# A two-layer decoder trunk: the second layer's gate is summed at the layer boundary, and the residual rows are made there

## Chip, cores and metric

The kernel runs on one core of a Trainium2 chip. The metric is the device time of one execution in microseconds (us), lower is better. TensorE (PE) does the matmuls, VectorE (DVE), ScalarE (ACT) and GpSimd (POOL) the element work, and SyncE's queue (SP) issues most transfers.

## What is computed

Two layers over one sequence of 1024 tokens of 1024 features. Each layer modulates its input by three rows made of a conditioning vector, projects it once for three groups of heads (latent attention A, dilated B, sparse C with an indexer), gates, projects back and normalizes:

```python
for l in range(DEPTH):
    mod = jax.nn.silu(c) @ w_ada[l] + b_ada[l]
    shift, scale, gate = jnp.split(mod, 3, axis=-1)
    h = x * (1.0 + scale[:, None, :]) + shift[:, None, :]
    (p_cq, p_ckv, p_kr, p_qb, p_kb, p_vb, p_qc, p_kc, p_vc,
     p_qi, p_ki, p_wi, p_gate) = jnp.split(h @ w_in[l], SPLIT_POINTS, axis=-1)
    ...
    y = jnp.concatenate([o_a, o_b, o_c], axis=-1) * jax.nn.silu(p_gate)
    sub = y @ w_out[l]
    x = layer_norm(ALPHA * x + (1.0 + gate[:, None, :]) * sub, ln_g[l], ln_b[l])
```

The gate is used only after the output projection of its layer. Layer 1's scale and shift are needed as layer 0's output is turned into layer 1's h.

## The kernel before

Every product is made of three or two matmuls on a high and a low part (`split_w` loads a weight tile, ACT rounds it to the high part, POOL subtracts for the low part, L196 to L198). h lies transposed in SBUF for the whole layer. A layer runs in this order in the code: `indexer` (keys of the indexer, then four query chunks, and the index scores, summed over eight heads by DVE into the tile `acc`), two latent projections, the dilated heads B with the other projections between them, `select` (a bitwise search for the 256th score on DVE and ACT), the sparse heads C, the latent attention `mla`, and `out_proj`. Before layer 1's `indexer` the values of its dilated heads are projected, token block by token block, from 7 down to 0 (`values_b` with `natural`).

Modulation. `begin` makes layer 0's scale and shift. The other four rows of numbers are made by `later(i, ring)`: i = 0 and 1 are the gates of layer 0 and 1, 2 and 3 layer 1's scale and shift. Each calls `ada`: a memset of an accumulator tile (from the ring G), a bias load, and eight times a load of 512 KB and a DVE multiply-add of 128x1024 (L261). A gate's accumulator is then summed over partitions by two half-row matmuls against ones, each copied out by ACT, and stored (`ada_row`, L273 to L275); scale and shift go through `part_sums` (L266). The list ADA says where in layer 0's indexer each one stands: ADA[0] ahead of the keys, ADA[1+j] behind the projection of query chunk j. Their weight loads use three buffers there (two pt, one bi).

Residual rows. Layer 1's residual is layer 0's normalized output times ln_g plus ln_b. `residual(i)` makes it for one token block: load x1_d into the single tile RES (L805), two POOL products of 128x1024 (L806, L807), store to xw_d (L808). The first one also loads LNG and LNB (L802, L803). The code calls it in `mla` of layer 1, two blocks behind each of the heads 0 to 3 (NRES). RES is also one of two buffers in which `out_proj` of layer 0 loads rows of x.

Order. The code's order is a rank, not the order of execution: the tile framework (`schedule_with_timeline_sim=True` in `kernel`) writes each engine's queue ahead of time by its own simulated clock, so an instruction far down in the code can stand early in a queue whose engine is free by that clock. On the chip each queue then runs strictly as written.

Slices of `acc` serve as buffers too: AC[0] to AC[3], 1024 columns each, hold rows in `out_proj` until their transposes (L890) have been read.

Of the kernel before, what the change touches and what calls it, by code (L numbers as in the profile page):

```python
# [8 lines left out]
F32 = mybir.dt.float32  # L9
# [13 lines left out]
NB = 8  # L23
# [20 lines left out]

NQ = ((2,2,3,4,6,6,6),(2,2,3,4,6,6,6))

ADA = ((0,),(1,),(2,),(3,),())

NPC = 2

# [10 lines left out]
KE = (1,1)  # L61

NPL = 2

NRES = ((0,0,0,0,0,0),(2,2,2,2,0,0))

EARLY = (2,2)
FB = ((0,2,4,0,2,0),(1,3,1,1,1,1))
# [40 lines left out]
def trunk(ctx: ExitStack, tc: tile.TileContext, a, out):  # L109
# [236 lines left out]
    def natural(tb, wk, n0, n, k0=0):  # L346

        ps = ps_p.tile([P, 512], F32, name="pj")
        tok = slice(tb * P, (tb + 1) * P)
        items = []  # L350
        for k, (wh, wl) in enumerate(wk):
            ah, al = HA[k0 + k]
            items += [(ah[:, tok], wh), (al[:, tok], wh), (ah[:, tok], wl)]
        chain(ps[:, :n], items)
        return ps
# [32 lines left out]
    def values_b(tb, ps):  # L388
        evac_v(ps, tb, 6, 0)
        dve.tensor_scalar(wi[:, tb, :], ps[:, 384:392], float(8 ** -0.5), 0.125, OP.mult, OP.mult)  # L390
# [293 lines left out]
    def mla(l, values):  # L684
        PR.tiles = PR3 + AC[1:4] + [AC[0]]
        place = [(4, 512), (4, 640), (3, 640), (4, 0), (3, 0), (2, 0), (1, 0), (0, 0)]
        turn = []
        for g in ORDA[l]:
            for qb in (2 * g, 2 * g + 1):
                if place[qb][0] not in turn:  # L690
                    turn.append(place[qb][0])

        def slots(h):

            rows = [PR.tiles[(5 * h + turn.index(i)) % len(PR.tiles)] for i, _ in place]
            return [r[:, o:o + (qb + 1) * P] for qb, (r, (_, o)) in enumerate(zip(rows, place))]


        s8 = [QK.next() for _ in range(8)]
        held[:] = s8  # L700
        KA = [s8[0:2], s8[4:6]]
        QA = Ring(s8[2:4] + s8[6:8])
        kr = WR.next()
        sp.dma_start(kr[64:96, :], kr_d)
        sp.dma_start(kr[96:112, :], kr_d[16:32, :])
        sp.dma_start(kr[112:128, :], kr_d[0:16, :])
        act.activation(KA[0][0][64:128, :], kr[64:128, :], AF.Copy)
        dve.tensor_tensor(KA[0][1][64:128, :], kr[64:128, :], bc(KA[0][0][64:128, :]), OP.subtract)
        for i in range(2):
            pool.dma_start(KA[1][i][0:64, :], KA[0][i][64:128, :])  # L710
        ct, kraw = BI.next(), BI.next()
        sp.dma_start(ct, a["rope"])
        RAW = Ring([scrf])

        def keys(p):
            wh, wl = split_w(a["wuk"][l, p], 256)

            def evac(half, cols, ps):
                dve.tensor_tensor(kraw[:, cols], ps, rb[half], OP.mult)
            project(wh, wl, 2, CK, evac)  # L720

        def key(h):
            e = h % 2
            rr = slice(0, 64) if e == 0 else slice(64, 128)
            act.activation(KA[e][0][rr, :], kraw[rr, :], AF.Copy)
            (pool if KE[l] else dve).tensor_tensor(KA[e][1][rr, :], kraw[rr, :], bc(KA[e][0][rr, :]), OP.subtract)

        def split_q(Q, raw, cols):
            act.activation(Q[0][:, cols], raw, AF.Copy)
            (dve if QE[l] else pool).tensor_tensor(Q[1][:, cols], raw, bc(Q[0][:, cols]), OP.subtract)  # L730

        def query(h):

            wh, wl = split_w(a["wuq"][l, h], 768)
            Q = [(QA.next(), QA.next()) for _ in range(2 if h == 4 else 1)]
            for e in range(len(Q)):
                q[h + e] = Q[e]

            def evac(half, cols, ps):
                c = ct[:, cols]  # L740
                for e in range(len(Q)):
                    raw = RAW.next()
                    n, r = (slice(64, 128), 0) if (h + e) % 2 else (slice(0, 64), 64)
                    own, other, both = slice(r, r + 32), slice(r + 32, r + 64), slice(r, r + 64)
                    if UE[l] & (1 if h < 4 else 2):
                        act.activation(raw[n], ps[n], AF.Copy)
                    else:
                        dve.tensor_copy(raw[n], ps[n])
                    if h < 2:
                        dve.tensor_tensor(raw[both], ps[both], c[both], OP.mult)  # L750
                    elif h < 4:
                        dve.tensor_tensor(raw[own], ps[own], c[own], OP.mult)
                        dve.tensor_tensor(raw[other], ps[own], c[other], OP.mult)
                    else:
                        sp.dma_start(raw[both], qr_d[both, cols])
                    split_q(Q[e], raw, cols)
                    if h in (2, 3):
                        t = RAW.next()
                        dve.tensor_tensor(t[own], ps[other], c[own], OP.mult)
                        dve.tensor_tensor(t[other], ps[other], c[other], OP.mult)  # L760
                        sp.dma_start(qr_d[both, cols], t[both])

            project(wh, wl, 6, CA, evac)

        q, y, rest = {}, {}, list(range(NB))
        keys(0)
        key(0)
        query(0)
        key(1)
        for i in range(1, NQ[l][0]):  # L770
            query(i)
        values(2, 4, 0)
        for h in range(6):
            if h % 2 == 0:
                y[h // 2] = G.next()
                sp.dma_start(y[h // 2], ga_d[h // 2])
            Kh, Kl = KA[h % 2]
            Qh, Ql = q[h]

            def done(g, yt=y[h // 2], yo=HA[h // 2], c=None):  # L780
                c = c or slice(g * 256, g * 256 + 256)
                act.activation(yo[0][:, c], yt[:, c], AF.Copy)
                pool.tensor_tensor(yo[1][:, c], yt[:, c], bc(yo[0][:, c]), OP.subtract)

            attend(f'A{h}', [(Qh, Kh), (Ql, Kh), (Qh, Kl)], vblk((h + 4) % 6), None, scq, y[h // 2],
                   (h % 2) * 64, ORDA[l], done if h in (3, 5) else None, PACK[l] and slots(h))
            if h < 4:
                if h % 2 == 0:
                    keys(h // 2 + 1)
                    if h == 2:  # L790
                        done(0, y[0], HA[0], slice(0, 1024))
                key(h + 2)
            for i in range(NQ[l][h], NQ[l][h + 1]):
                if i < 5:
                    query(i)
            for _ in range(NRES[l][h]):
                residual(rest.pop(0))

    def residual(i):

        if i == 0:
            sp.dma_start(LNG, a["ln_g"][0].to_broadcast([P, 1024]))  # L802
            sp.dma_start(LNB, a["ln_b"][0].to_broadcast([P, 1024]))  # L803
        tb = TBO[i]
        sp.dma_start(RES, x1_d[tb])  # L805
        pool.tensor_tensor(RES, RES, LNG, OP.mult)  # L806
        pool.tensor_tensor(RES, RES, LNB, OP.add)  # L807
        sp.dma_start(xw_d[tb], RES)  # L808
# [159 lines left out]
    for l in range(DEPTH):  # L968
        layer[0] = l
        indexer(l)  # L970
        jobs = [lambda i=i: latent(l, i) for i in range(8)] + [lambda i=i: gate_a(l, i) for i in range(3)]
        values = None
        rb.clear()

        def fill_b(h):
            for _ in range(FB[l][h]):
                jobs.pop(0)()

        def fill_c(h):
            nonlocal values  # L980
            for _ in range(FC[l][h]):
                jobs.pop(0)()
            if h == 1:
                assert not jobs
                values = latents_back(l)

        for _ in range(EARLY[l]):
            jobs.pop(0)()
        heads_bc(l, BQK, 6, GB, 3, fill_b)
        select(l)  # L990
        if NPC:
            PR.tiles = PR.tiles + [BI.tiles[1], BI.tiles[0]][:NPC]
        heads_bc(l, CQK, 4, GC, 6, fill_c, extra=lambda: values_c(l))
        mla(l, values)
        out_proj(l)
        if l + 1 < DEPTH:
            wv = stage_vb(l + 1, Ring(held[4:8] + PT.tiles + [fresh("pr2", F32R), fresh("pr1", F32R)]))
            for tb in TBO:
                values_b(tb, natural(tb, wv, 0, 392))
            PR3[1:] = [fresh(f"pr{i}", F32) for i in (1, 2)]  # L1000
            PR.tiles = PR3[:]
            BI.tiles[1] = fresh("bi1", F32)
            RW.tiles = [fresh(f"rw{i}", F32, 512) for i in range(2)]
            G.tiles = [fresh(f"g{i}", F32) for i in range(2)]


def consts():
# [78 lines left out]
```

## Time and profile before

| | us |
|---|---|
| median of 3 runs | 1750.54 (1749.58 to 1754.23) |
| the profiled execution's own time | 1750.43 |
| its span, first to last instruction | 1748.6 |
| PE busy | 1673.0 (96%) |
| DVE busy | 1350.5 (77%) |
| ACT busy | 1019.8 (58%) |
| POOL busy | 666.9 (38%) |
| mean granted TensorE clock | 0.985 |

All rows below are of that execution; times in them are us from the span's start. The first layer's index stage runs from about 62 to 200, the layer boundary lies at about 896, and the second layer's index stage runs from 935 to 1055.

### The profile page before, as it was taken

To read this page: it belongs to the slowest core of one execution; us is meant where nothing else is said; L and a number is where in the kernel's file an instruction comes from. 1 tells how busy PE (TensorE), PEld (TensorE's weight loads), DVE (VectorE), ACT (ScalarE), POOL (GpSimd) and SP (SyncE) were. 2 spreads that over 40 slices of the span, in tenths; PEclk is the share of its full clock that TensorE was granted. 3 is DMA by queue.
4 is the path that set the end of the run, shared out by engine and by line. 5 is a ranking of instruction groups with operands and counts; after the bars stand their busy time and mean duration, and the time that the engine had idled before them with its cause. 6 is when DMAs were issued, how large, how long until landed. Compare 5 with 4: busy or idle time off the path is not lost.

```text
span 1748.6 us, 26930 instructions
## 1 busy us (share of the span) xinstructions
PE 1673.0 (96%) x9192; PEld 1451.5 (83%) x9192; DVE 1350.5 (77%) x3213; ACT 1019.8 (58%) x2010; POOL 666.9 (38%) x614
## 2 busy tenths in 40 slices
PE   8999899999999999989999999999999899998998
PEld 8888688888887888878898977888789788987886
DVE  6888898888588678885772668889876967778777
ACT  4254599895534666675112656999744357667620
POOL 0221143323434355463346413333243344657421
PEclk9999999999999999999999999999999999999999
DMA  9665023233202521222343421333221227113122
GB/s 367 212 215 189 25 73 97 70 136 91 79 35 54 221 90 58 73 70 93 125 157 124 168 73 49 85 111 95 73 97 50 60 52 265 47 52 124 49 86 95
DMA packets 57668, 187.32 MB, mean 107 GB/s; under 512 B 7862, under 2 KB 8886, under 8 KB 57020
## 3 DMA queue, kind: packets, MB, share of 16 engines
q1 hardware_dynamic: 53116, 156.25, 26.3%
q0 software_dynamic: 4416, 29.36, 5.8%
q8 instruction: 72, 1.18, 0.3%
q14 instruction: 64, 0.52, 0.1%
HBM read 133.94 MB, written 39.07 MB: 99 GB/s over the span
## 4 chain that ended last, share of the span: by engine, by line
PE 53%; DVE 8%; ACT 3%; issue 2%; DMA 1%; POOL 1%; DVEq 0%; ACTq 0%; POOLq 0%
PE pj L204 30%; PE S L204 12%; PE O L332 5%; PE T L320 5%; DVE pt L324 1%; ACT pt L323 1%; PE T L204 1%; ACT scr L485 1%; DVE acc L543 0%; DVE pr L536 0%; DVE acc L441 0%; PE T L890 0%; DVE h L818 0%; DVE acc L291 0%; ACT pr L296 0%
## 5 line engine op out<-in xcount | busy, mean ns | idle before, releaser
L204 PE MATMUL pj<-h,w 128*128 128x512 f32 (+1 forms) x3408 | 833.0, 391 | 13.9 <-DVE qk L238 5.8
L204 PEld LDWEIGHTS pj<-h,w 128*128 128x128 f32 x3408 | 629.9, 190 | 131.1 <-issue 11.9
L198 POOL TENSOR_TENSOR w<-wr,w 128x1024 fp32r<-128x1024 f32 (+2 forms) x86 | 192.4, 2238 | 302.3 <-ACT w L197 290.1
L204 PE MATMUL S<-qk,qk 128*128 128x512 f32 (+2 forms) x1104 | 279.7, 358 | 8.4 <-DVE mx L288 3.1
L323 ACT ACTIVATE pt<-T 128x512 fp32r<-128x512 f32 (+1 forms) x320 | 172.4, 551 | 111.2 <-PE T L320 53.8
L298 POOL TENSOR_SCALAR pr<-pr,den 128x896 f32<-128x896 f32 (+7 forms) x180 | 139.0, 776 | 253.3 <-DVE den L297 223.9
L324 DVE TENSOR_TENSOR pt<-T,pt 128x512 fp32r<-128x512 f32 (+1 forms) x320 | 199.5, 633 | 43.9 <-ACT pt L323 37.9
L332 PE MATMUL O<-pt,v 128*128 128x256 f32 (+1 forms) x1280 | 212.8, 286 | 9.2 <-DVE pt L324 4.1
L485 ACT ACTIVATE scr<-acc,U 128x768 uint8<-128x768 f32 x186 | 193.2, 1038 | 35.6 <-DVE U L481 18.1
L204 PEld LDWEIGHTS S<-qk,qk 128*128 128x128 f32 x1104 | 184.2, 190 | 33.4 <-DVE mx L288 6.4
L332 PEld LDWEIGHTS O<-pt,v 128*128 128x128 f32 x1280 | 186.1, 191 | 26.7 <-DVE pt L324 6.7
L339 POOL TENSOR_TENSOR g<-g,osum 64x256 f32<-64x256 f32 x128 | 98.9, 773 | 235.0 <-DVE osum L337 222.8
L296 ACT ACTIVATE pr<-pr,mx 128x384 f32<-128x384 f32 (+7 forms) x188 | 145.5, 775 | 48.1 <-DVE mx L288 31.2
L320 PE MATMUL T<-ident,pr 128*128 128x128 f32 x852 | 145.4, 279 | 6.3 <-POOL pr L298 3.1
L467 DVE TENSOR_SCALAR_CACHE_REDUCE scr<-acc,U 128x384 uint8<-128x384 f32 x186 | 138.2, 743 | 3.8
L197 ACT ACTIVATE w<-wr 128x1024 fp32r<-128x1024 f32 (+2 forms) x86 | 83.8, 976 | 69.2 <-PE pj L204 59.7
L320 PEld LDWEIGHTS T<-ident,pr 128*128 128x128 f32 x852 | 102.1, 142 | 18.7 <-POOL pr L298 4.2
L204 PE MATMUL pj<-w,h 128*128 128x256 f32 (+2 forms) x672 | 107.0, 300 | 0.2 <-ACT w L835 0.2
L204 PEld LDWEIGHTS pj<-w,h 128*128 128x128 f32 x672 | 91.7, 190 | 5.1 <-ACT w L835 0.5
L336 ACT ACTIVATE osum<-O 64x256 f32<-64x256 f32 x128 | 48.6, 380 | 63.4 <-PE O L332 60.3
L441 DVE SCALAR_TENSOR_TENSOR acc<-S,wi,acc 128x512 f32<-128x512 f32 (+1 forms) x84 | 55.7, 678 | 23.0 <-ACT S L436 22.8
L337 DVE TENSOR_TENSOR osum<-O,osum 64x256 f32<-64x256 f32 x128 | 53.5, 418 | 25.1 <-ACT osum L336 21.4
(282 smaller groups left out, 2512.2 us busy)
## 6 DMA issues: line engine op xcount, KB each, us to landing
wr<-in_wt_dram SPq DMA_DIRECT2D x62, 512.0 KB, 3.9
cq_d<-rw SPq DMA_DIRECT2D x64, 256.0 KB, 2.0
h<-cq_d POOLq DMA_DIRECT2D x4, 4096.0 KB, 19.1
qk<-qk POOLq DMA_DIRECT2D x48, 256.0 KB, 3.0
pt<-in_w_ada_dram SPq DMA_DIRECT2D x22, 512.0 KB, 4.7
wr<-in_w_out_dram SPq DMA_DIRECT2D x16, 512.0 KB, 3.5
bi<-in_bias_dram SPq DMA_DIRECT2D x14, 512.0 KB, 3.7
bi<-in_w_ada_dram SPq DMA_DIRECT2D x10, 512.0 KB, 4.4
```

The source lines that it names most:

```text
L197: act.activation(hi[:, :n], raw[:, :n], AF.Copy)
L198: (lo_eng or pool).tensor_tensor(lo[:, :n], raw[:, :n], bc(hi[:, :n]), OP.subtract)
L204: pe.matmul(ps, lhsT=l, rhs=r, start=(i == 0), stop=(i == len(items) - 1))
L296: act.activation(p[:, :n], p[:, :n], AF.Exp, bias=m, scale=-1.0, accum_out=den)
L298: (dve if ne[qb] else pool).tensor_scalar(p[:, :n], p[:, :n], den, 0.5, OP.mult, OP.mult)
L320: pe.transpose(t[:, c:c + P], p[j](2 * kp + kk), ident)
L323: act.activation(pt[:, 0, :n], t[:, :n], AF.Copy)
L324: dve.tensor_tensor(pt[:, 1, :n], t[:, :n], bc(pt[:, 0, :n]), OP.subtract)
L332: pe.matmul(o[:, oc], lhsT=vt(kb), rhs=pt[:, e, pc], start=(kb == 0 and e == 0), stop=(kb == 2 * g + 1 and e == 1), skip_group_check=True)
L339: pool.tensor_tensor(yc, yc, s[r0:r0 + 64], OP.mult)
L467: dve.tensor_scalar(scr8[:, :IDX_LEN[b]], scores(b), s, None, op, OP.add, accum_out=dst[:, b:b + 1])
L485: act.activation(scr[:, :IDX_LEN[b]], scores(b), AF.Sign, bias=U[:, b:b + 1].bitcast(F32), accum_out=cnt[:, b:b + 1])
```

## The change

Layer 0's gate moves from ahead of the indexer's keys to behind the first query chunk, where layer 1's gate was. Layer 1's gate moves out of layer 0 altogether: it is summed after layer 1's dilated values, with AC as its ring of four buffers, ahead of layer 1's indexer. The residual rows are made there as well, one token block behind each block of values, and no longer in `mla`. The G tiles are taken anew one statement earlier, so that `later(1)` has an accumulator.

```diff
-ADA = ((0,),(1,),(2,),(3,),())
+ADA = ((),(0,),(2,),(3,),())
...
-NRES = ((0,0,0,0,0,0),(2,2,2,2,0,0))
...
-        q, y, rest = {}, {}, list(range(NB))
+        q, y = {}, {}
...
-            for _ in range(NRES[l][h]):
-                residual(rest.pop(0))
...
-            for tb in TBO:
+            for i, tb in enumerate(TBO):
                 values_b(tb, natural(tb, wv, 0, 392))
+                residual(i)
+            G.tiles = [fresh(f"g{i}", F32) for i in range(2)]
+            later(1, Ring(AC))
             PR3[1:] = [fresh(f"pr{i}", F32) for i in (1, 2)]
             PR.tiles = PR3[:]
             BI.tiles[1] = fresh("bi1", F32)
             RW.tiles = [fresh(f"rw{i}", F32, 512) for i in range(2)]
-            G.tiles = [fresh(f"g{i}", F32) for i in range(2)]
```

## Rows read from the trace of the kernel before

**Rows 1.** The page, part 1: busy us, share of the span, instructions.

```profile
PE 1673.0 (96%) x9192; PEld 1451.5 (83%) x9192; DVE 1350.5 (77%) x3213; ACT 1019.8 (58%) x2010; POOL 666.9 (38%) x614
```

**Rows 2.** Busy time by stretch; columns as in the first line.

```profile
core 0: us, PE busy (x) PEld busy (x) DVE busy (x) ACT busy (x) POOL busy (x), PEclk, DMA share, GB/s
61.80:200.27 138.47, 128.43 (x624) 108.18 (x625) 122.00 (x175) 63.33 (x127) 26.17 (x13) 0.97 0.53 169
935.00:1055.00 120.00, 113.50 (x563) 99.04 (x562) 70.40 (x123) 60.47 (x119) 47.22 (x23) 0.99 0.35 119
...
185.00:200.20 15.20, 10.22 (x42) 5.88 (x41) 14.82 (x30) 9.14 (x20) 2.77 (x2) 0.87 0.13 40
1040.00:1055.00 15.00, 9.52 (x42) 5.83 (x41) 14.15 (x29) 8.62 (x19) 2.96 (x2) 0.93 0.16 46
...
82.00:95.00 13.00, 10.33 (x42) 8.31 (x43) 9.37 (x12) 3.58 (x6) 4.94 (x3) 0.87 1.01 296
...
919.00:962.00 43.00, 40.99 (x217) 38.08 (x216) 11.37 (x23) 9.48 (x17) 25.43 (x15) 1.00 0.39 128
```

**Rows 3.** Timeline of PE, first index stage: start, us, instruction [idle before <-releaser].

```profile
82.27 1.02 PE L273 MATMUL O<-g,ones 128*1 128x512 f32 x2 [0.80 <-DVE g L261]
85.69 5.80 PE L204 MATMUL pj<-h,w 128*128 128x384 f32 x23 [2.40 <-DVE pr L409]
...
109.19 4.05 PE L204 MATMUL pj<-h,w 128*128 128x384 f32 x22 [0.50 <-DVE qk L231]
```

**Rows 4.** The modulation sums and their loads: durations min/median/max, then landing.

```profile
L261 DVE SCALAR_TENSOR_TENSOR g<-pt,cs,g x22: 1271/1285/3314, 63.2 to 158.2; 128x1024 f32<-128x1024 f32 x22
...
DMA to landing us min/median/max: 3.4/4.4/8.1
```

**Rows 5.** Timeline of DVE, both index stages.

```profile
76.45 5.77 DVE L261 SCALAR_TENSOR_TENSOR g<-pt,cs,g 128x1024 f32<-128x1024 f32 x2
82.14 1.27 DVE L261 SCALAR_TENSOR_TENSOR g<-bi,cs,g 128x1024 f32<-128x1024 f32 x1
83.44 0.69 DVE L238 TENSOR_TENSOR qk<-pj,qk 64x512 fp32r<-64x512 f32 x1
84.17 0.68 DVE L408 TENSOR_TENSOR rw<-pj,bi 32x512 f32<-32x512 f32 x1
84.86 0.68 DVE L409 TENSOR_TENSOR pr<-pj,bi 32x512 f32<-32x512 f32 x1
...
101.01 0.91 DVE L256 MEMSET g<- 128x1024 f32 x1 [0.16 <-issue]
...
961.89 0.62 DVE L439 TENSOR_SCALAR acc<-T,wi 128x384 f32<-128x384 f32 x1 [0.24 <-ACT T L436]
```

**Rows 6.** Timeline of PE at the layer boundary.

```profile
918.82 0.49 PE L890 MATMUL T<-ident,acc 128*128 128x128 f32 x3
...
926.52 2.39 PE L204 MATMUL pj<-qk,h 128*128 128x392 f32 x12 [0.98 <-DVE wi L390]
928.75 1.24 PE L204 MATMUL pj<-pt,h 128*128 128x392 f32 x6
...
959.26 0.41 PE L204 MATMUL T<-qk,qk 128*128 128x384 f32 x1 [0.85 <-DMA qk<-qk]
```

**Rows 7.** Timeline of POOL, first index stage and layer boundary.

```profile
78.28 2.86 POOL L198 TENSOR_TENSOR w<-wr,w 128x1024 fp32r<-128x1024 f32 x1 [0.49 <-ACT w L197]
...
952.90 2.41 POOL L807 TENSOR_TENSOR res<-res,lnb 128x1024 f32<-128x1024 f32 x1
955.26 0.55 POOL L242 DMA_DIRECT2D qk<-qk  x1
```

**Rows 8.** SP's queue: two issues, and its longest wait from 895 to 995.

```profile
33.70 0.43 SPq L802 DMA_DIRECT2D lng<-in_ln_g_dram  x1
...
899.26 0.33 SPq L805 DMA_DIRECT2D res<-x_d  x1
...
SPq L808 <- POOL res L807: 49.6, 8, 8.3
```

## The prediction, before the change was run

> **What bounds the kernel now.** I read the page's first part, then the busy time by stage, then the timelines of the two places that the change touches. TensorE is busy for 1673.0 of 1748.6 us [rows 1]: it runs at its peak almost everywhere, so a change that leaves its work alone can only win back its idle time and the time it runs at a lower granted clock, or add to them. The diff adds no matmul and drops none: two rows of two half-row sums change places. All else that moves (VectorE sums, loads, GpSimd's residual products) lies beside TensorE. So I ask, for each place: what does TensorE wait for there now, and will it wait longer or less?
>
> The two index stages are nearly the same work, and only the first one has the four modulation sums in it. The first stage (61.80 to 200.27) leaves TensorE idle for 138.47 - 128.43 = 10.0 us at a clock of 0.97; the second (935 to 1055) for 120.00 - 113.50 = 6.5 us at 0.99 [rows 2]. With the clock counted as lost time (0.03 x 138.5 = 4.2 us against 0.01 x 120 = 1.2 us), all four sums together cost (10.0 - 6.5) + (4.2 - 1.2) = 6.5 us of stalls. This is the most that the first place can give. The tail of the stage is no part of it: TensorE idles 15.20 - 10.22 = 5.0 us from 185 on, and 15.00 - 9.52 = 5.5 us in the same tail of layer 1, where no sum runs [rows 2].
>
> The stalls that belong to the sums stand at the head of the stage. At 82.27 TensorE waits 0.80 us for the last sum of layer 0's gate, at 85.69 2.40 us for VectorE to empty the second half of the keys' projection (L409), and the 23 matmuls behind that take 5.80 us, 0.252 each, where a later run of the same shape takes 4.05/22 = 0.184 [rows 3]: (0.252 - 0.184) x 23 = 1.6 us more. The clock granted in 82 to 95 is 0.87 of 2.4 GHz, a mix with its lower level of 1.2 GHz, and what went before is that idle time [rows 2]. Together 0.8 + 2.4 + 1.6 = 4.8 us of the 6.5.
>
> **The change, part by part.** *Layer 0's gate is no longer first in the index stage.* later(0) keeps its 8 multiply-adds, one memset, 8 weight loads, bias load, two half rows and store, but is ranked behind the keys and the first index queries; later(1), as large, leaves the stage. VectorE there loses 8 x 1.285 + 0.91 = 11.2 us [rows 4, 5] of 122.00 busy in 138.47 [rows 2]. That much would matter if VectorE set the pace; but the tail is the same without sums (above), so what can go is the head's 4.8 us. Does it go? The keys' second evacuation (L238 at 83.44) stood behind three sums: two from 76.45 on, 5.77 us together, and one at 82.14 [rows 5]. Six sums stand ahead of 76.45 in that timeline, so the one at 82.14 is the ninth, that is the first of later(1), which the code already ranks behind the keys. So rank did not decide that order: the planner writes the queues by its own clock, and by that clock the keys were not ready yet. With later(0) in later(1)'s place the same sums may be written ahead of the same evacuation. Bounds: 0 (the order stays) and 6.5 us (the stage loses all that layer 1's does not have). I take half of the head, 2.4 us, because the evidence for either order is one row.
>
> *Layer 1's gate goes to the layer boundary.* 8 multiply-adds and a memset, 11.2 us of VectorE; ten transfers on SP's queue; two half rows, 1.02 us each, on TensorE [rows 3], which left the first stage, so they cancel. Cover: from 919 to 962 VectorE is busy for 11.37 of 43 us [rows 2], so 31.6 us are free. Their four weight buffers are slices of the index scores; three of these hold the last rows of out_proj until their transposes end at 918.82 + 0.49 = 919.3 [rows 6], so the second load can start about there, lands 4.4 us later (the median) [rows 4], and the sums, two rounds of four buffers, end by about 919.3 + 2 x 4.4 + 7 x 1.285 = 937. The scores are written from 961.89 on [rows 5]: 25 us of slack. Queued behind a waiting sum on VectorE are the values' evacuations of the last three or four token blocks; TensorE waits for such a one already, 0.98 us at 926.52 [rows 6]. The half rows can wait for the last sum as the earlier ones did, 0.80 us [rows 3]. Bounds: below nothing by 1.8 us (the 0.98 there and the 0.85 at 959.26 vanish [rows 6]), above by the slower rival. I take 0.8 us, the wait that the same instruction had in layer 0.
>
> A sum that runs beside a GpSimd operation is longer: the longest took 3.314 us against a median of 1.285 [rows 4], while GpSimd worked from 78.28 to 81.14 [rows 7]. At the boundary sixteen GpSimd products of about 2.4 us run beside the eight sums. At 3.31 each they are 26.5 us, still under the 31.6 free. The Trainium skill, SBUF — State Buffer, "Who interferes with whom", has the rule: a VectorE instruction with two SBUF inputs and a GpSimd instruction that reads SBUF take one shared port in turn, and the later one waits for the whole of the other. It speaks against this change, and the 3.314 us agrees with it. By it the eight sums cost up to 8 x 2.4 = 19 us more of VectorE, 30 of 31.6 us, and evacuations would stand behind them, which is an ingredient of the slower rival and no end of my range.
>
> *The residual products move from layer 1's latent attention to the boundary.* In the code that is far earlier; in the trace it is nothing: their first load is issued at 899.26 already, and LNG, which the same function loads, at 33.70 [rows 8]. The first cannot start sooner, since out_proj reads its RES tile until then. So 16 loads and stores and 16 products stay where they are and only rise in rank. Behind them on GpSimd stand the index weights' low parts and the keys' copy: one product at 952.90 stands directly ahead of the copy at 955.26 [rows 7], and TensorE waits 0.85 us for it at 959.26 [rows 6]. Bounds: -0.85 and one more product, +2.4 us. I take 0: one already stands there.
>
> The sum, against the profiled execution's own time: 1750.43 - 2.4 + 0.8 + 0 = 1748.8 us. That time is 1.8 us above its span and 0.1 below the median of 1750.54, so it needs no shift.
>
> **Rivals.** *The order does not follow the code.* The planner placed the residual products far ahead of the code's place, and one sum ahead of work that outranks it. Then gate 0's sums run where they run now, the head's stall stays, and the boundary hides the rest: 1750.4. For it: 82.14 and 899.26. Against: VectorE does lose 11.2 us.
>
> *The head clears.* The keys are emptied when they are done, the queries follow without a stall, the clock stays up, and the boundary costs nothing: 1750.4 - 6.5 to -4.8 = 1743.9 to 1745.6, and with the boundary's own 1.8 us gone 1742.1. I take 1744.5. For it: layer 1's stage. Against: three of four sums stay in layer 0's.
>
> *The boundary's sums stop TensorE (slower).* SP stands at each residual store until GpSimd is done, 49.6 us over eight, at most 8.3 [rows 8]. A weight load queued behind such a store comes that much late; VectorE, in order, stands at the sum, and the evacuation behind it cannot run. TensorE has two banks there, so one block's 24 matmuls as cover, about 4.5 us (12 of them from 926.52 to 928.75, 2.23 us) [rows 6]. Each such event costs 8.3 - 4.5 = 3.8 us and 1.6 us of lower clock as in the head: 5.4. One makes 1750.4 - 2.4 + 5.4 = 1753.4, still no change; from two on it is slower: 1758.8. For it: the store waits, and a sum of 3.3 us. Against: the planner knows of these waits and writes loads that are ready ahead of the store; VectorE is a quarter busy there.
>
> **How the numbers follow.** Forecast 1748.8, chance 0.38; order unchanged, 1750.4, 0.15; the head clears, 1744.5, 0.25; boundary stops TensorE, 1758.8, 0.22. What this kernel's measurement can tell from no change is about 0.3%, 5.25 us, so 1745.3 to 1755.8 is "same": the first two cases, 0.53. Faster 0.25 and slower 0.22 are the others. The range goes from 1742.0 (all stalls of the stage and of the boundary gone) to 1759.0 (two events, rounded up); beyond it lies about a tenth on each side, from a shifted plan of the later stages.
>
> **What would show it.** Right: VectorE's busy time from 62 to 200 falls by some 11 us, the tail's 5 us of idle stay, the residual loads still begin near 899 less the gain, and the sums at the boundary end 20 us ahead of the first score. The head: is L238 for the keys' second half ahead of the seventh sum, and is 0.87 gone? Wrong: TensorE idle between 919 and 962 over 4 us with a wait for VectorE or for the half row's sum; a copy of the keys behind two products; or a stage far from both places whose idle time differs by more than 3 us.

## The result: 1.4% slower, and most of it far from the two places that the change touches

The changed kernel took 1777.28 us (1772.36 to 1777.98), the kernel before beside it 1751.17 us (1749.58 to 1754.23): a ratio of 1.0138, 95% interval 1.0122 to 1.0154. The forecast was 1748.8 us and its range ended at 1759. In the changed kernel a line has a number that is lower by 2 in the first half of the file and by 4 behind `mla` (L261 is L259 there, L390 is L388, L806 is L802).

The work is the same; TensorE, VectorE and the span are all longer [rows 1]. Page of the changed kernel, part 1:

```profile
PE 1684.9 (95%) x9192; PEld 1461.4 (82%) x9192; DVE 1362.0 (77%) x3213; ACT 1022.5 (58%) x2010; POOL 664.0 (37%) x614
```

Where the 27 us are is read from four marks in TensorE's timeline: the start of the last transposes (L619) of each layer's index stage, the first matmul of the dilated values (out_proj has ended), and the first matmul of layer 1's indexer keys. Counted from 61.80 us on, they cut the span into five stretches. Busy time by stretch, the changed kernel first (the last two lines are the head and the tail of the first index stage), then the kernel before, cut at its own marks; columns as in [rows 2]:

```profile
61.80:199.65 137.85, 126.22 (x617) 109.40 (x617) 109.79 (x165) 63.70 (x125) 26.04 (x13) 0.96 0.43 139
199.65:916.66 717.01, 684.51 (x3756) 586.57 (x3757) 559.94 (x1396) 433.90 (x864) 281.10 (x277) 0.97 0.28 89
916.66:962.17 45.51, 40.20 (x226) 38.68 (x224) 30.02 (x38) 8.72 (x16) 24.32 (x13) 0.96 0.58 200
962.17:1081.81 119.64, 114.18 (x560) 98.01 (x560) 72.90 (x125) 60.90 (x120) 47.05 (x23) 0.99 0.37 121
82.00:95.00 13.00, 10.44 (x42) 8.42 (x43) 9.76 (x12) 3.57 (x6) 5.26 (x3) 0.87 1.02 303
185.00:200.08 15.08, 10.01 (x45) 6.78 (x44) 13.64 (x28) 9.61 (x19) 2.94 (x2) 0.87 0.11 37
```

```profile
61.80:199.77 137.97, 127.93 (x621) 107.69 (x622) 121.53 (x174) 63.33 (x127) 26.17 (x13) 0.97 0.52 169
199.77:896.23 696.46, 672.40 (x3757) 578.76 (x3756) 551.88 (x1395) 433.80 (x864) 283.99 (x277) 0.99 0.28 91
896.23:935.15 38.92, 37.94 (x225) 37.47 (x224) 19.16 (x32) 7.83 (x15) 23.16 (x13) 1.00 0.42 151
935.15:1053.92 118.77, 112.27 (x557) 97.83 (x557) 69.35 (x122) 60.47 (x119) 47.22 (x23) 1.00 0.34 119
```

Read the second number of each line, the length. The first index stage gains 0.1 us. The rest of layer 0, where no line that runs there was changed, loses 717.01 - 696.46 = 20.5 us. The boundary loses 6.6, layer 1's index stage 0.9, and what follows gains 0.9. In the rest of layer 0 TensorE's idle time (length less busy) goes from 24.1 to 32.5 us, and the same 3756 or 3757 matmuls are busy for 12.1 us more, at a granted clock of 0.97 for 0.99. VectorE does the same 1396 or 1395 instructions there in 559.94 us for 551.88.

Two of the larger new stalls of that stretch are these. Timeline of the changed kernel (columns as in [rows 3]), first around 525, then around 745 us:

```profile
522.67 2.93 DVE L541 SCALAR_TENSOR_TENSOR acc<-scr,bi 128x640 f32<-128x640 uint8 x1
525.64 2.58 DVE L530 TENSOR_SCALAR scr<-acc,thr 128x768 uint8<-128x768 f32 x1
528.14 0.41 DVE L362 TENSOR_TENSOR v<-pj,v 128x256 fp32r<-128x256 f32 x1
...
522.53 5.27 POOL L196 TENSOR_TENSOR w<-wr,w 128x1024 fp32r<-128x1024 f32 x2 [6.19 <-ACT w L195]
...
528.61 7.65 PE L202 MATMUL pj<-h,w 128*128 128x512 f32 x21 [3.88 <-DVE v L362]
...
742.88 2.69 DVE L728 TENSOR_TENSOR qk<-scr,qk 128x512 fp32r<-128x512 f32 x1 [1.07 <-ACT qk L727]
...
742.63 2.38 POOL L724 TENSOR_TENSOR qk<-bi,qk 64x1024 fp32r<-64x1024 f32 x1
...
748.47 1.06 PE L202 MATMUL S<-qk,qk 128*128 128x512 f32 x3 [4.06 <-DVE pr L292]
```

The same two mask instructions and the products of that time in the kernel before:

```profile
515.76 0.81 DVE L543 SCALAR_TENSOR_TENSOR acc<-scr,bi 128x640 f32<-128x640 uint8 x1
516.61 0.62 DVE L532 TENSOR_SCALAR scr<-acc,thr 128x768 uint8<-128x768 f32 x1
...
510.91 2.40 POOL L198 TENSOR_TENSOR w<-wr,w 128x1024 fp32r<-128x1024 f32 x1 [0.60 <-ACT w L197]
524.64 2.85 POOL L198 TENSOR_TENSOR w<-wr,w 128x1024 fp32r<-128x1024 f32 x1 [1.97 <-ACT w L197]
...
524.67 5.72 PE L204 MATMUL pj<-h,w 128*128 128x512 f32 x24 [2.63 <-DVE qk L238]
```

In the changed kernel GpSimd makes two weights' low parts while VectorE does the two mask instructions: these take 2.93 and 2.58 us, where 0.81 and 0.62 are enough when GpSimd stands still. Behind them on VectorE stands the evacuation that TensorE needs, and TensorE waits 3.88 us. At 742 it is the same with another product of GpSimd, 2.69 us where the twelve of its kind in before have a median of 0.69, and TensorE waits 4.06 us, of which this makes 2.0. The kernel before has such meetings too, but others and shorter.

At the boundary two things are seen. Timeline of the changed kernel:

```profile
914.84 0.91 DVE L254 MEMSET g<- 128x1024 f32 x1 [0.35 <-PE pj L202]
...
918.17 2.05 DVE L259 SCALAR_TENSOR_TENSOR g<-acc,cs,g 128x1024 f32<-128x1024 f32 x1 [0.61 <-DMA g<-in_b_ada_dram]
920.14 0.68 DVE L865 SCALAR_TENSOR_TENSOR pr<-res,pr 128x512 f32<-128x512 f32 x1
...
953.53 7.95 DVE L259 SCALAR_TENSOR_TENSOR g<-acc,cs,g 128x1024 f32<-128x1024 f32 x3
...
961.94 3.91 DVE L259 SCALAR_TENSOR_TENSOR g<-acc,cs,g 128x1024 f32<-128x1024 f32 x3
...
942.39 0.49 PE L886 MATMUL T<-ident,acc 128*128 128x128 f32 x3
...
946.31 0.62 PE L202 MATMUL pj<-pt,h 128*128 128x392 f32 x2 [2.90 <-POOL h L375]
...
962.17 5.70 PE L202 MATMUL pj<-h,w 128*128 128x512 f32 x24 [1.51 <-DVE wi L388]
...
942.36 2.67 POOL L803 TENSOR_TENSOR res<-res,lnb 128x1024 f32<-128x1024 f32 x1
945.00 1.26 POOL L375 TENSOR_TENSOR h<-g,h 128x512 fp32r<-128x512 f32 x1
...
954.35 2.71 POOL L802 TENSOR_TENSOR res<-res,lng 128x1024 f32<-128x1024 f32 x1 [5.24 <-DMA res<-x_d]
957.14 3.26 POOL L803 TENSOR_TENSOR res<-res,lnb 128x1024 f32<-128x1024 f32 x1
```

First, the memset and the first sum stand among the steps of the last token block's layer norm (L864 to L866), which everything at the boundary waits for: its last transposes begin at 942.39, 25.7 us after out_proj's end, where they began 918.82 - 896.23 = 22.6 us after it [rows 6]. Behind them GpSimd's part of h (L375) stands after a residual product, and TensorE waits 2.90 us for it, a wait that the kernel before does not have. Second, three sums beside two residual products take 7.95 us, three without such company 3.91 (1.30 each). In the 7.95 us the sum that began ahead of the first product takes 1.28, and the two that began beside one 3.30 each. A copy of the values' last columns (L388) stands behind each three, and TensorE waits 1.51 us for the one behind the first three.

### The profile page after: what moved, and what is told of

It is laid out like the page before. It is cut to its first block, busy times and chain, and to the rows that moved or that the text cites. A ratio compares the mean times of both kernels' runs of the same rounds, so it can differ in the third digit from the quotient of the medians.

```text
span 1775.6 us, 26938 instructions
## 1 busy us (share of the span) xinstructions
PE 1684.9 (95%) x9192; PEld 1461.4 (82%) x9192; DVE 1362.0 (77%) x3213; ACT 1022.5 (58%) x2010; POOL 664.0 (37%) x614
## 4 chain that ended last, share of the span: by engine, by line
PE 63%; DVE 18%; ACT 9%; issue 4%; DMA 4%; POOL 1%; SPq 0%; DVEq 0%; ACTq 0%; POOLq 0%
PE pj L202 35%; PE S L202 13%; PE O L330 6%; PE T L318 5%; ACT scr L483 4%; DVE scr L465 2%; DVE g L259 2%; DVE pt L322 2%; DVE acc L439 1%; ACT pt L321 1%; ACT pr L294 1%; PE T L202 1%; DVE pr L286 1%; PE S L907 1%; DVE qk L236 1%
## 5 line engine op out<-in xcount | busy, mean ns | idle before, releaser
L202 PE MATMUL pj<-h,w 128*128 128x512 f32 (+1 forms) x3408 | 842.3, 394 | 21.0 <-DVE qk L236 6.6
L202 PEld LDWEIGHTS pj<-h,w 128*128 128x128 f32 x3408 | 636.4, 192 | 141.2 <-issue 16.8
L296 POOL TENSOR_SCALAR pr<-pr,den 128x896 f32<-128x896 f32 (+7 forms) x180 | 138.3, 772 | 273.6 <-DVE den L295 226.1
L465 DVE TENSOR_SCALAR_CACHE_REDUCE scr<-acc,U 128x384 uint8<-128x384 f32 x186 | 138.3, 744 | 3.9
L434 ACT ACTIVATE S<-S 128x512 f32<-128x512 f32 (+1 forms) x96 | 49.7, 525 | 41.6 <-PE S L202 40.7
```

The source lines that it names most:

```text
L202: pe.matmul(ps, lhsT=l, rhs=r, start=(i == 0), stop=(i == len(items) - 1))
L296: (dve if ne[qb] else pool).tensor_scalar(p[:, :n], p[:, :n], den, 0.5, OP.mult, OP.mult)
L465: dve.tensor_scalar(scr8[:, :IDX_LEN[b]], scores(b), s, None, op, OP.add, accum_out=dst[:, b:b + 1])
```

## The experiments

Lengths of the stretches in us, from the marks named above, of the profiled execution of each kernel. Median and ratio are of all its times against the kernel before.

| kernel | first index stage | rest of layer 0 | boundary | index stage of layer 1 | rest of span | median | ratio (95%) |
|---|---|---|---|---|---|---|---|
| before | 138.0 | 696.5 | 38.9 | 118.8 | 694.7 | 1751.2 | |
| changed | 137.9 | 717.0 | 45.5 | 119.6 | 693.8 | 1777.3 | 1.0138 (1.0122 to 1.0154) |
| e1_gate_twice | 137.9 | 696.2 | 46.1 | 119.6 | 696.3 | 1761.2 | 1.0066 (1.0044 to 1.0088) |
| e2_keep0 | 136.1 | 713.5 | 45.5 | 119.6 | 696.1 | 1777.2 | 1.015 (1.013 to 1.017) |
| e3_rank | 139.2 | 695.6 | 38.9 | 119.0 | 694.3 | 1752.3 | 1.0006 (0.9995 to 1.0017) |
| e4_parity | 133.9 | 696.1 | 46.0 | 119.6 | 696.8 | 1756.5 | 1.0034 (1.0021 to 1.0047) |
| e5_flip | 138.3 | 699.6 | 38.9 | 119.2 | 693.4 | 1752.5 | 1.0006 (0.9993 to 1.002) |
| e6_draw_first | 140.2 | 695.7 | 45.4 | 119.6 | 694.3 | 1758.2 | 1.0035 (1.0018 to 1.0052) |
| e7_ring3 | 136.1 | 696.3 | 42.0 | 121.3 | 695.9 | 1754.6 | 1.0018 (1.0006 to 1.0029) |
| e8_small_products | 136.6 | 696.0 | 47.2 | 119.0 | 689.6 | 1751.2 | 1.0001 (0.999 to 1.0011) |
| e9_three_first | 136.5 | 697.1 | 45.9 | 119.6 | 691.0 | 1756.3 | 1.0026 (1.0014 to 1.0037) |
| e10_gate_in_stage | 138.5 | 698.3 | 38.9 | 130.6 | 694.7 | 1760.0 | 1.0053 (1.0039 to 1.0066) |
| e11_gate_late | 139.3 | 696.2 | 38.9 | 129.4 | 693.7 | 1760.7 | 1.005 (1.0037 to 1.0063) |
| e12_mended | 137.9 | 697.0 | 41.7 | 124.7 | 696.2 | 1760.6 | 1.0054 (1.004 to 1.0069) |

All diffs are against the kernel before unless another is named. The gate's statement at the boundary is the same in all that have it:

```diff
 (behind the loop over the values' token blocks)
+            G.tiles = [fresh(f"g{i}", F32) for i in range(2)]
+            later(1, Ring(AC))
```

**e1_gate_twice** adds that statement, with one draw from G behind it, and leaves ADA as it was: all four sums stay in the first stage, and layer 1's gate is summed a second time at the boundary.

> Layer 0 as before with all four sums in its index stage, and layer 1's gate summed a second time at the layer boundary. Its TensorE queue is the one of the kernel before up to the last token blocks of layer 0's output projection. Replan theory (layer 0 lost 20 us because the planner wrote another order for it once a sum had left): layer 0's output projection ends near 896 as before, the boundary takes some 45.5 us instead of 39.0, total 1757 to 1760 us. Boundary theory (the sums at the boundary are the loss, wherever the trace books it): 1773 to 1778 us.

The boundary is 46.1 us and layer 0 is as before: the sums at the boundary cost 7.2 us, and they don't cost layer 0 anything.

**e2_keep0** moves layer 1's gate and leaves layer 0's where it was, without the residual rows:

```diff
-ADA = ((0,),(1,),(2,),(3,),())
+ADA = ((0,),(),(2,),(3,),())
```

> Layer 1's gate leaves layer 0 for the boundary, layer 0's gate stays ahead of the keys, the residual rows stay where they were in the code. Replan theory: a third order for layer 0, whose end lies anywhere from 885 to 925 us and need not be 916; total 1745 to 1785. Removal theory (taking 11.2 us of VectorE out of the index stage slows layer 0 as such, for instance because what follows comes earlier and collides): layer 0's output projection ends at 912 to 920 as in the changed kernel, total 1773 to 1778 us.

713.5 us in layer 0 and 1777.2 in all, the changed kernel's time. Neither layer 0's gate nor the residual rows are needed for the loss; here one sum that leaves the first stage is enough.

**e3_rank** is the other half alone: all four sums stay, layer 0's gate is listed behind the keys.

```diff
-ADA = ((0,),(1,),(2,),(3,),())
+ADA = ((),(0,),(1,),(2,),(3,))
```

> All four sums stay in layer 0, each one query chunk later in the code, so that none stands ahead of the keys; nothing moves to the boundary. Removal theory: nothing has left, 1747 to 1753 us. Replan theory: another order again, 1740 to 1775 us. Head theory of the prediction (the keys are emptied sooner): the 2.4 us wait of TensorE for L409 is gone and the stage ends some 5 us ahead of 200.

The time does not change, nor does the stage get shorter (139.2 for 138.0), and TensorE still waits 2.40 us for L409 at 85.50: a lower rank alone does not clear the head.

**e4_parity** has the changed kernel's gate, and draws the next tile of G in the place where layer 1's gate was summed, so that the sums and gates behind it have the same of the two tiles as before.

```diff
-ADA = ((0,),(1,),(2,),(3,),())
+ADA = ((),(0,1),(2,),(3,),())
...
-                later(i, more)
+                later(i, more) if i != 1 else G.next()
```

> As the changed kernel without the residual move, but one accumulator tile is drawn and left unused in layer 0, so that its gates use the same of the two G tiles as before the change. Tile theory (layer 0 lost 20 us because its gates and the output projection swapped the two G tiles): layer 0 ends near 896 again, total 1755 to 1760 us. Removal theory: 1773 to 1778 us. Replan theory: a fourth order, 1745 to 1785 us.

Layer 0 is 696.1 us: the whole 20.5 us are gone, by a draw that computes nothing. It changes two things, the tile that each gate has and which sum must wait for which, so three kernels tell these apart from the order of the queues.

**e5_flip** exchanges the tiles alone; every queue holds the same instructions in the same order as before.

```diff
-        indexer(l)
+        indexer(l); G.n += 1 - l
...
-            G.tiles = [fresh(f"g{i}", F32) for i in range(2)]
+            G.tiles = [fresh(f"g{i}", F32) for i in range(2)]; G.n += 1
```

> The kernel before, with only the two tiles that the sums and gates draw in turn exchanged from the end of layer 0's first index stage on; every engine keeps its order of instructions. The changed kernel exchanges them too, since it takes one draw out of that stage. Theory A, the 20.5 us that layer 0 lost after that stage lie in another order of the work: here 199.8 to 896 stays 696 us long, 1751 us in all. Theory B, they lie in which of the two tiles a gate has: 713 to 717 us, 1768 to 1772 us in all.

699.6 us in layer 0 (3.1 more than before in the profiled execution) and a ratio of 1.0006: the 20.5 us are not the tiles.

**e6_draw_first** throws the draw away ahead of all sums (`ADA = ((),(0,),(2,),(3,),())`, the gate at the boundary, and):

```diff
-        more = Ring(PT.tiles + ([BI.next()] if l == 0 else []))
+        G.n += 1 - l; more = Ring(PT.tiles + ([BI.next()] if l == 0 else []))
```

> The gate's sums at the boundary as in the changed kernel, the other three sums in the first index stage, with one draw of the two tiles thrown away ahead of all of them, where e4_parity threw it away between the first and the second. The gates then have the tiles they have in e4_parity, but no sum waits for the one before the last to be read, as e4_parity's do. Theory tiles, it is the tiles that a gate has: 200 to the end of layer 0 is 696 us, 1756 to 1761 us in all. Theory position, it is where the remaining sums come to stand and what the rest of the order makes of it: between 700 and 717 us, 1762 to 1777 us in all, with stalls like the changed kernel's at 283 to 288 and 427 us if it is the same order.

695.7 us. No sum waits here for the tile of the one just ahead of it, and layer 0 is whole. By its words this is the theory of the tiles; e5_flip has ruled that one out, and what this kernel shares with e4_parity is the order of most of layer 0's queues (below).

**e9_three_first** has the gate at the boundary and no draw at all. The remaining sums are only listed one place earlier than the changed kernel has them:

```diff
-ADA = ((0,),(1,),(2,),(3,),())
+ADA = ((0,),(2,),(3,),(),())
```

> The gate's sums at the boundary as in the changed kernel; the three that stay are listed first, second and third of the stage (the changed kernel lists them second, third and fourth), with no draw thrown away. GpSimd's queue of layer 0 comes out with the weights' low parts where before has them; the changed kernel's has them behind softmax normalisations. Theory order, the 20.5 us of layer 0 lie in that order: 200 to the end of layer 0 is 695 to 698 us, 1755 to 1761 us in all. Theory three sums, any layer 0 with three sums in the stage and no sum waiting for another's tile loses them: 713 to 717 us, 1772 to 1778 us in all.

Rest of layer 0, busy time by stretch: first e9_three_first, then e2_keep0.

```profile
198.25:895.38 697.13, 672.54 (x3756) 577.84 (x3757) 552.94 (x1396) 434.51 (x864) 283.29 (x277) 0.99 0.28 91
```

```profile
197.85:911.38 713.53, 680.87 (x3756) 584.10 (x3757) 559.69 (x1396) 433.79 (x864) 281.33 (x277) 0.98 0.27 89
```

Three sums in the stage as in the changed kernel, the same instructions in layer 0, the same tile of G for every sum and gate as in e2_keep0, and the loss is absent: TensorE idles 24.6 us against 32.7, and VectorE needs 552.94 us against 559.69. What differs is the order in which the planner wrote the queues.

This order can be read from the traces, instruction by instruction (line, operation, tiles, shape). In every kernel that takes a sum out of the stage, or only lists one later (e3), the start of layer 0 is ordered otherwise than before. In those without a loss TensorE's queue soon comes back to that of before: from 291 us on (e3, e6; times of before) or 332 (e4) to the boundary, and in e9 and e12 from 369 on, 2164 matmuls in a row, with one more stretch of another order from 750 to 767. GpSimd's queue comes back likewise. In the changed kernel and in e2_keep0, whose TensorE queues of layer 0 are the same but for the place of three matmuls, it stays another until GpSimd's comes back at 779, ScalarE's at 791, VectorE's at 801 and TensorE's at 817. In places GpSimd has the weights' low parts (L198) and the keys' copies (L241, L242) behind softmax normalisations (L298) that they stood ahead of.

The loss has grown where the orders differ, and grows no more once they agree. Counted from the end of the first index stage in each kernel, it is 6.5 us by the low part at 344.89 (in the changed kernel at 351.25), 20.8 us where TensorE's queue has come back, and 20.5 at out_proj's end. The kernel before, then the changed kernel, behind that place:

```profile
818.16 1.21 PE L332 MATMUL O<-pt,v 128*128 128x256 f32 x5 [0.41 <-DVE osum L337]
```

```profile
838.87 1.21 PE L330 MATMUL O<-pt,v 128*128 128x256 f32 x5 [0.30 <-DVE osum L335]
```

So the cause of the loss in layer 0 is the plan, which a small shift in the first stage turned over and which in these two kernels came back only near the end of the layer. Which engine's order does it alone was not tried; the two stalls shown above are the parts of it that were traced to their source.

The residual rows' new place in the code changes nothing at the boundary: from out_proj's end to 1096 us, beyond layer 1's index stage, the changed kernel and e2_keep0, which has the rows where they were, run the same instructions in the same order on TensorE, VectorE, ScalarE and GpSimd, and the boundary takes 45.5 us in both. What that place does further down in layer 1 was not tested by itself.

**e7_ring3** asks what the boundary pays for. It is e4_parity with three buffers, so that the first sum doesn't come ahead of the last layer norm (against e4_parity):

```diff
-            later(1, Ring(AC))
+            later(1, Ring(AC[1:4]))
```

> e4_parity, with the boundary's four column reads going through three buffers in place of four, so that the first sum doesn't stand in the layer norm of the last token block of layer 0's end. Theory first, that sum is what sets the boundary back: the stretch from the end of layer 0 to the keys falls from 45.95 to 42.5 to 43.5 us, 1753 us in all. Theory port, VectorE's sums and GpSimd's residual products slow each other and that is what the stretch pays: it stays at 45 to 46 us, 1756 us.

42.0 us, 3.9 less than e4_parity: the sum in the layer norm's chain was more than half of the boundary's loss. The wait for GpSimd's part of h (2.87 us in e4_parity) is gone; in its place TensorE waits 2.98 us for a copy (L390) behind a sum whose slice has not landed. 1.7 us come back in layer 1's index stage.

**e8_small_products** is e4_parity with the residual products on 8 columns (most of the residual's scale and shift is left out; against e4_parity):

```diff
-        pool.tensor_tensor(RES, RES, LNG, OP.mult)
-        pool.tensor_tensor(RES, RES, LNB, OP.add)
+        pool.tensor_tensor(RES[:, :8], RES[:, :8], LNG[:, :8], OP.mult)
+        pool.tensor_tensor(RES[:, :8], RES[:, :8], LNB[:, :8], OP.add)
```

> e4_parity, with GpSimd's two residual products, which run at the boundary beside the sums, cut to 8 columns: most of the residual's scale and shift is left out. Theory port: the sums take 1.28 us each, as in the index stage of before, in place of 2.65, the copy of the keys waits 2 to 4 us less, and the boundary is 42 to 43.5 us in place of 45.95, 1752.5 to 1754 us in all. Theory first, the sum in the layer norm's chain sets it: it stays at 45 to 46 us, 1756 us. If both hold, each of e7_ring3 and this gets a part of the 7 us that e4_parity has over before.

Timeline of e8_small_products (SPq is SyncE's queue):

```profile
921.44 0.32 SPq L808 DMA_DIRECT2D xw_d<-res  x1
921.85 1.73 SPq L260 DMA_DIRECT2D acc<-in_w_ada_dram  x3
...
927.84 2.63 DVE L261 SCALAR_TENSOR_TENSOR g<-acc,cs,g 128x1024 f32<-128x1024 f32 x2 [3.76 <-DMA acc<-in_w_ada_dram]
...
930.86 0.15 DVE L390 TENSOR_SCALAR wi<-pj 128x8 f32<-128x8 f32 x1
...
931.47 3.92 DVE L261 SCALAR_TENSOR_TENSOR g<-acc,cs,g 128x1024 f32<-128x1024 f32 x3
...
931.16 4.12 PE L204 MATMUL pj<-qk,h 128*128 128x392 f32 x12 [4.62 <-DVE wi L390]
```

The price of a sum is as the port theory has it: 1.31 us each, in twos and threes, once GpSimd's long products are gone (only the first, in the layer norm's chain, takes 2.18). The boundary gets no shorter for it, 47.2 us: now VectorE stands 3.76 us at a sum whose slice has not landed, with an evacuation and a copy (L364, L390) behind it that TensorE needs, and TensorE's one wait for the copy is 4.6 us. The slices' loads (L260) are issued right behind a residual store (L808), 4.2 us after the last transposes have ended (917.67). But this kernel does not test the length alone: the planner wrote another order here too (TensorE's differs from that of e4_parity from 911 us on). It shows that sums at their short price can still hold TensorE up by their place ahead of the evacuations; what the short price would save in the order of e4_parity is not shown. Its total equals that of before because the span behind layer 1's index stage is 5 us shorter; why was not followed up.

**e10_gate_in_stage** and **e11_gate_late** try for a version that beats before: e4_parity, with layer 1's gate in layer 1's own index stage, behind the first or the third chunk of queries, in the two transpose buffers:

```diff
+        if l == 1:
+            PT.tiles = [fresh(f"pt{i}", F32) for i in range(2)]
...
-            for i in ADA[1 + j] if l == 0 else ():
-                later(i, more)
+            for i in ADA[1 + j] if l == 0 else ((1,) if j == 0 else ()):
+                later(i, more) if i != 1 or l else G.next()
```

(e11 has `j == 2`; neither has the statement at the boundary.)

> e4_parity, with layer 1's gate summed in layer 1's own index stage, behind its first indexer queries, into the two buffers of the transposes, which are idle there; nothing of it stands at the boundary. Theory boundary, what e4_parity has over before is paid at the boundary, where VectorE's sums wait for their slices ahead of the keys' copies: the boundary is 38.5 to 39.5 us as in before, the index stage of layer 1 grows by less than 1 us from 118.8 us since VectorE is busy 6 parts in 10 there, the first stage keeps 1.4 to 4.1 us, and the whole takes 1746.5 to 1750 us. Rival, the eight sums cost wherever they stand while TensorE is the bound: layer 1's stage pays 4 to 7 us, 1753 to 1757 us.

> As e10_gate_in_stage, but behind the third pair of indexer heads' queries in place of the first. Theory boundary: the same time as e10_gate_in_stage within 2 us, 1746.5 to 1750 us; if the first places beside the keys are what VectorE lacks, this one is the faster by 1 to 3 us. Theory order: layer 1's later stages come out in another order in the two, so either can lose some us from 1054 on that have nothing to do with the sums.

The boundary is 38.9 us again, as before, and layer 1's index stage pays 10.7 to 11.9 us in its place, more than either theory gave it. Timeline of e10_gate_in_stage (its L411 is L409 of before):

```profile
941.59 4.29 DVE L261 SCALAR_TENSOR_TENSOR g<-pt,cs,g 128x1024 f32<-128x1024 f32 x2 [2.72 <-DMA pt<-in_w_ada_dram]
948.13 1.28 DVE L261 SCALAR_TENSOR_TENSOR g<-pt,cs,g 128x1024 f32<-128x1024 f32 x1 [2.25 <-DMA pt<-in_w_ada_dram]
949.44 0.69 DVE L238 TENSOR_TENSOR qk<-pj,qk 64x512 fp32r<-64x512 f32 x1
...
951.67 5.99 PE L204 MATMUL pj<-h,w 128*128 128x384 f32 x24 [3.06 <-DVE pr L411]
966.74 5.77 PE L204 MATMUL pj<-h,w 128*128 128x384 f32 x24 [4.36 <-DVE qk L231]
```

It is the head of the first stage over again [rows 3, 5]: VectorE waits 2.25 us for a slice, the keys' evacuation (L238) waits behind it, and TensorE waits 3.06 and then 4.36 us, with 24 matmuls at 0.25 and 0.24 us behind each where a later run takes 0.184 [rows 3]. Moving the sums later in the code did not move this wait: in e11_gate_late VectorE waits 2.27 us for a slice ahead of the same evacuation, and TensorE 3.36 us.

**e12_mended** is the changed kernel with e9's listing and e7's three buffers:

```diff
-ADA = ((),(0,),(2,),(3,),())
+ADA = ((0,),(2,),(3,),(),())
...
-            later(1, Ring(AC))
+            later(1, Ring(AC[1:4]))
```

> The changed kernel whole, residual rows included, with two edits: the three sums that stay are listed as in e9_three_first, whose queues of layer 0 it shares, and the boundary's sums use three buffers as in e7_ring3. If the changed kernel's 27 us are the order of layer 0 (20.5 us) and the boundary (6.6 us, of which the first sum in the layer norm's chain is 3.9 us), it takes 1777.3 - 20.5 - 3.9 = 1753 us, 1751 to 1756 us: 200 to the end of layer 0 is 695 to 698 us, the boundary 41.5 to 42.5 us. If the residual rows' new place had a part in the loss, layer 0 or the boundary stays longer and it is above 1758 us.

Layer 0 (697.0) and boundary (41.7) came as expected, and the time did not: layer 1's index stage took 124.7 us, where e7_ring3 took 121.3 and e4_parity 119.6. Rows of e12_mended, then one of e7_ring3:

```profile
954.73 2.39 POOL L198 TENSOR_TENSOR w<-wr,w 128x1024 fp32r<-128x1024 f32 x1
957.07 0.61 POOL L241 DMA_DIRECT2D qk<-qk  x1
...
945.32 1.02 PE L273 MATMUL O<-g,ones 128*1 128x512 f32 x2 [1.20 <-DVE g L261]
968.38 0.44 PE L204 MATMUL T<-qk,qk 128*128 128x384 f32 x1 [2.01 <-DMA qk<-qk]
```

```profile
964.37 0.44 PE L204 MATMUL T<-qk,qk 128*128 128x384 f32 x1 [1.42 <-DMA qk<-qk]
```

The copies of the keys (L241, L242) are issued behind residual products and a weight's low part, the first score waits 2.01 us for them, and the granted clock of 965 to 980 is 0.89. The order is not new: over the boundary and layer 1's index stage the four engines of e7_ring3 run the same instructions in the same order. There the half row of the gate does not wait (1.20 us here), the score waits 1.42 us, and the clock of 965 to 980 is 1.00. Since e7_ring3 has the residual rows left in `mla`, the rows' place in the code has no part in this order. So the two mends do not add up: with three buffers the index stage of layer 1 pays part of what the boundary gains, and in this kernel it paid more than in e7_ring3. Why it did so with the same order stays open.

## Why the prediction was wrong, step by step

*The rest of layer 0: a term that the sum did not have.* The step that failed is the last sentence on the range, where a shifted plan of the later stages was left outside with a tenth on each side. The same text had two rows that showed the planner not following the code (a sum at 82.14, the residual loads at 899.26) and drew from it only that a step may stay where it is. It did not draw that a step which does move lets everything behind it be ordered anew: layer 0's 697 us, with VectorE 79% busy, were taken as fixed. The new order cost +20.5 us there, three quarters of the result. The list of signs had it ("a stage far from both places whose idle time differs by more than 3 us": 8.4).

*The first index stage: -2.4 forecast, -0.1 measured.* VectorE's busy time fell by 11.7 us (11 forecast) and the tail still idles 5.1 us, as the text said. The head did not move. Timeline of the changed kernel:

```profile
82.17 1.02 PE L271 MATMUL O<-g,ones 128*1 128x512 f32 x2 [0.70 <-DVE g L259]
85.58 6.00 PE L202 MATMUL pj<-h,w 128*128 128x384 f32 x24 [2.40 <-DVE pr L407]
```

These are the stalls of [rows 3] to within 0.1 us, and the clock of 82 to 95 is 0.87 in both. The rival "the order does not follow the code" described this place. Over the ten kernels with one gate less in the stage its length went from -4.1 to +2.2 us against before, -0.7 in the mean: half of the head was too much.

*The boundary: +0.8 forecast, +6.6 measured* (7.2 in e1_gate_twice, where it stands alone). The slack ahead of the scores was right (the last sum ends at 965.85, VectorE's first step on a score starts at 989.97: 24 us, 20 forecast), and so was the longer sum beside GpSimd. The failed step is the cover: 31.6 free us of VectorE say nothing of where in its queue a sum stands. The text let the second load start at the transposes' end and did not ask where the sum of the first slice, which is free earlier, would stand; and it named the evacuations behind a sum but priced them at nothing, for its 0.8 us are the half row's wait. In fact that first sum came into the layer norm's chain (3.9 us by e7_ring3), and later ones held up a copy (1.51 us). The slower rival had the right victim, the evacuation behind a sum. Its cause, a slice that is late behind a residual store in SP's queue, is seen in e8_small_products; in the changed kernel only the first sum waits for a transfer, 0.61 us for its bias.

The rule of the Trainium skill that was quoted (SBUF — State Buffer, "Who interferes with whom") agrees with the runs as to the price: 3.30 us for each of the two sums begun beside the products, 1.28 to 1.31 without. What that price costs the boundary is not shown: in e8_small_products it was gone and the boundary not shorter, but its order was another.

*The residual rows: 0 forecast*, and at the boundary nothing is seen of their new place in the code, since e2_keep0 has the same order and length there without it. The first load follows out_proj's end by 4.4 us (3.0 before), at 921.10. *The half rows* cancel as reckoned: TensorE is busy for 1.7 us less in the first stage and for 1.9 us more in layer 1's.

So the sum 1750.43 - 2.4 + 0.8 + 0 should have been 1750.4 - 0.1 + 20.5 + 6.6 + 0.9 - 0.9 = 1777.4, the last two terms being layer 1's index stage and what follows it.

## What to carry to other kernels

Where a planner writes the queues, an edit's cost is not only at its place: look at the stages behind it, and once it has been made, compare the order of an engine's queue there before explaining the time. An engine with free time is no cover by itself; on an engine that runs in order, ask which instruction stands behind the added one and who waits for that, above all if the added one waits for a transfer. A loss that comes from a plan can be taken back by a change without meaning (a listing, a thrown away draw), but such mends need not add up: e9 alone took 1756.3 us, and e12, which adds e7's buffers to it, 1760.6.

## What was not expected of the hardware

A short wait of TensorE can cost more behind it than itself, and not in every execution. In before, TensorE waits 2.63 us at 524.67 and its next 24 matmuls take 5.72 us, 0.238 each. e9_three_first has the same wait at the same place:

```profile
525.13 8.62 PE L204 MATMUL pj<-h,w 128*128 128x512 f32 x24 [2.62 <-DVE qk L238]
```

Its 24 matmuls take 0.359 us each, 2.9 us more in all, and the granted clock of 525 to 535 is 0.69. In the changed kernel the first 21 matmuls behind the wait of 3.88 us take 7.65, 0.364 each, and the granted clock of 515 to 535 is 0.83, between its levels of 1.2 and 2.4 GHz. Over the rest of layer 0 this is the larger part of the loss: 8.4 us of idle time came with 12.1 us of slower work. Why the clock falls after one wait and not after an equal one these runs don't tell.
